# Encoder trunk on one core: sink negation moved behind the tables, tables begun with the third chunk of x, first slab cast first, products of zeros at the start

## The chip, the core and the metric

The kernel runs on one core of a Trainium2 chip. Time is device time in microseconds (us) of one execution; three executions of the kernel before gave 1385.47, 1386.06 and 1386.40 us, a median of 1386.06 us. One more execution was profiled.

Names used below: PE is TensorE's matmul side and PEld its weight loads; DVE is VectorE, ACT is ScalarE, POOL is GpSimd, SP is SyncE. Each engine works through its own instructions in the order in which the program issues them. DMAs are issued from queues of SP, ACT and POOL.

## What is computed

```python
def reference(x, positions, attn_norm_g, w_in, ..., w_down):       # x: (1, 512, 1024) float32
    cos, sin = rope_tables(positions)
    for l in range(2):
        h = rms_norm(x, attn_norm_g[l])
        z = jnp.einsum('bsd,dc->bsc', h, w_in[l])                  # 1024 -> 4352 columns
        qa, ka, va, qb, kb, vb, ga, gb = jnp.split(z, IN_SPLITS, axis=-1)
        ...                                                        # q/k norms, rope on the A branch
        ya = window_gqa(qa, ka, va, sink_a[l]) @ w_proj_a[l]       # softmax with a sink value per head
        yb = neighbourhood_attn(qb, kb, vb, rel_bias_b[l]) @ w_proj_b[l]
        x = x + (sigmoid(ga) * ya + sigmoid(gb) * yb) @ w_out[l]
        h = rms_norm(x, ffn_norm_g[l])
        x = x + (silu(h @ w_gate[l]) * (h @ w_up[l])) @ w_down[l]
    return x
```

## The kernel before

Every large product is made of three products in a reduced float32 format: an operand is cut into a high part and a low part, and high times high, high times low and low times high are added in PSUM. One such product with 512 moving columns is the unit of PE's work. ACT makes a high part (a copy with rounding), DVE makes the low part (a subtraction).

x is held in eight **chunks** of 128 columns of the model width (`KD = 8`), the weights in **slabs** of some rows and columns. Layer 0 begins with `token_matmul` (line 881) for the A queries: for each chunk k it calls `start(nrm, k)` through `begin`, and then makes the 12 products of that chunk (four blocks of tokens `b`, three products each). `begin(k+1)` is called right after the three products of block 0 of chunk k, so PE's order is: four transposes of chunk 0; three products (chunk 0, block 0); four transposes of chunk 1; nine products (chunk 0, blocks 1 to 3); three products (chunk 1, block 0); four transposes of chunk 2; and so on.

`start` (line 1174) for one chunk issues: four transposes of `xin[k]` on PE into a bank `at`; `first_parts(k)`, the cut of the weight rows of that chunk (ACT cast to the high part, DVE subtraction to the low part); an ACT activation that reads the transposes and gives the high part `nrm.xh[k]`; an ACT copy of them to `xT[k]`; a DVE operation (SCALAR_TENSOR_TENSOR) from `xT[k]` to the low part `nrm.xl[k]`; an ACT square and a DVE addition for the mean square. For chunk 0, `first_parts` stands behind the activation to `xh`; for all others ahead of it. The three products of block 0 need, in this order, (xh, weight high), (xh, weight low) and (xl, weight high).

The first slab (chunks 0 and 1) is loaded by ACT's queue in two halves, the next three slabs by POOL's queue (`first_load`, line 529); x is loaded chunk by chunk by SP's queue. POOL's queue carries, in this order, the positions, the B gains, slab 1, further B gains, slabs 2 and 3, the A gains `gqa`, the sink values `snk`, the rest of the constants `cst`, and then later slabs.

Beside the main order of the products run **chains**: generators with conditions (`Need`), issued whenever a dry run of the whole program (with a cost for each operation) finds the operands ready and the engine's backlog under a limit. The dry run thereby sets the order of instructions on each engine; the second run replays it. `issue` and `drive` (lines 394 and 413) do this at every yield of the main order. `chain_tables` (line 751) makes the rope tables: it converts the positions into `vec2`, negates the sink values into `nsnk`, transposes `vec2` on PE, forms angles from `cst`, and makes two tables `trig` by Sin on ACT, the first with a load of ACT's function table; all else is DVE work in small pieces. `chain_rope_tables` (line 789) then needs `trig` and `gqa`. `nsnk` is read first by the A heads' score operations.

`mm_bank()` gives PSUM banks in a rotation of four, `at_bank()` those of another four. The PE instruction with which the program begins is the transpose of `vec` (gains of the norms), then the transposes of chunk 0.

Of the kernel before, what the change touches and what calls it, by code (L numbers as in the profile page):

```python
# [12 lines left out]
F32 = mybir.dt.float32  # L13
# [3 lines left out]
ALU = mybir.AluOpType  # L17
AX = mybir.AxisListType

P = 128  # L20
# [4 lines left out]
NB = S // P  # L25
# [61 lines left out]
def by_columns(ap):  # L87

    return ap.rearrange("p (r cc c) -> p cc r c", r=8, c=8)


def held(ap):
    return ap.rearrange("p (cc r c) -> p cc r c", r=8, c=8)
# [116 lines left out]
def trunk(ctx: ExitStack, tc: tile.TileContext, a: dict, out: bass.AP, lay: Layout):  # L210
    nc = tc.nc
    PS = bass.MemoryType.PSUM
    cp = ctx.enter_context(tc.tile_pool(name="cp", bufs=1))
# [7 lines left out]
    def nm(s):  # L221
        uid[0] += 1
        return f"{s}_{uid[0]}"
# [21 lines left out]
    def act(dtype=F32):  # L245
        return buf([S], dtype)

    def mm_bank():
        return pm.tile([P, S], F32, tag="mm", name=nm("mm"))

    def at_bank():
        return pa.tile([P, S], F32, tag="at", name=nm("at"))
# [42 lines left out]
    def touch(aps, start, end):  # L295
        for x in aps:
            o = name_of(x)
            if isinstance(o, int):
                lay.touch(o, steps[0], start, end)

    class Engine:
# [3 lines left out]
        def __getattr__(self, name):  # L305
            f = getattr(self.eng, name)

            def call(*args, **kw):
                if not lay.dry:
                    f(*args, **kw)  # L310
                    return
                aps = [x for x in (*args, *kw.values()) if isinstance(x, bass.AP)]
                acc = kw.get("accum_out") if "accum_out" in kw else (args[7] if name == "tensor_tensor_reduce" else None)
                steps[0] += 1
                sources = aps if kw.get("start") is False else aps[1:]
                start = max([clock[self.key]] + [at_(name_of(x), self.key) for x in sources])
                if self.key == "dma":
                    start = max(start, clock["pe"] - 3.0)
                    if self.eng is nc.gpsimd:
                        clock["pool"] += 1.0  # L320
                    end = start + aps[0].free_size() * aps[0].shape[0] * 4 / 360e3
                    clock["dma"] = end
                    end += 2.0 if aps[1].space == bass.MemoryType.DRAM else 7.0
                    ready[name_of(aps[0])] = end, "dma"
                    touch(aps, start, end)
                    return
                end = start + cost(self.key, name, aps[0], aps)
                clock[self.key] = end
                ready[name_of(aps[0])] = end, self.key
                if acc is not None:  # L330
                    ready[name_of(acc)] = end, self.key
                touch(aps, start, end)

            return call

    T = Engine(nc.tensor, "pe")
    V = Engine(nc.vector, "dve")
    A = Engine(nc.scalar, "act")
    G = Engine(nc.gpsimd, "pool")
# [44 lines left out]
    chains, done = [], set()  # L384
# [156 lines left out]
    def first_parts(k):  # L541
        raw, h, lo = raws[k // 2][:, k % 2], highs[k // 2][:, k % 2], lows[k // 2][:, k % 2]
        A.copy(h, raw)
        V.tensor_tensor(lo, raw, h.bitcast(F32), ALU.subtract)
# [149 lines left out]
    vec2T = cp.tile([P, P], F32, tag="vec2T", name="vec2T")  # L694
    ones = cp.tile([P, 2], F32, tag="ones", name="ones")
    magic = cp.tile([P, 32], I32, tag="magic", name="magic")
    G.memset(vec2, 0.0)
    G.memset(ones, 1.0)
    G.memset(magic, 0x5F3759DF)
# [15 lines left out]
    posi = cp.tile([P, P], I32, tag="posi", name="posi")  # L715
# [14 lines left out]
    gqa = cp.tile([P, 2, DEPTH, HD], F32, tag="gqa", name="gqa")  # L730
    for i, n in enumerate(("q_norm_a", "k_norm_a")):
        GQ.dma_start(gqa[:, i], a[n].rearrange("l d -> (l d)").unsqueeze(0).to_broadcast([P, DEPTH * HD]))
    snk = cp.tile([P, DEPTH, 8], F32, tag="snk", name="snk")
    GQ.dma_start(snk, a["sink_a"].rearrange("l h -> (l h)").unsqueeze(0).to_broadcast([P, DEPTH * 8]))
    GQ.dma_start(cst[:, P:], a["consts"][:, P:])
    warm = cp.tile([P, 2], F32, tag="warm", name="warm")
    A.copy(warm, ones)
    ps = at_bank()
    T.transpose(ps[:, :32], vec, ident[:32, :32])
    V.tensor_copy(vecT, ps[:, :32])  # L740

    def gain(norm, k):
        c = 16 * (norm % 2) + 8 * (norm // 2) + k
        return vecT[:, c : c + 1]

    xT = [buf([S]) for _ in range(KD)]
    nsnk = cp.tile([P, DEPTH, 8], F32, tag="nsnk", name="nsnk")
    gb = cp.tile([P, DEPTH], F32, tag="gb", name="gb")
    trig = cp.tile([P, 2, NB, 32], F32, tag="trig", name="trig")

    def chain_tables():
        yield Need("dve", [posi, snk, gqa])
        V.tensor_copy(vec2[64:68], posi[64:68])
        V.tensor_scalar(nsnk, snk, -1.0, None, ALU.mult)
        yield Need("pe", [vec2], [at_slots])
        at_slots.take()
        ps = at_bank()
        T.transpose(ps[:, :P], vec2, ident)
        yield Need("dve", [ps])
        V.tensor_copy(vec2T, ps[:, :P])  # L760
        at_slots.give(clock["dve"])
        posf = vec2T[:, 64:68]
        V.scalar_tensor_tensor(gb, vec2T[:, 0:2], HD ** -0.5, vec2T[:, 2:4], ALU.mult, ALU.mult)
        v3 = lambda t: t[:, : NB * 32].rearrange("p (b f) -> p b f", b=NB)
        ang = v3(act())
        for b in range(NB):
            V.tensor_scalar(ang[:, b, :], cst[:, C_INV : C_INV + 32], posf[:, b : b + 1], None, ALU.mult)
        yield Need()
        for i, shift in enumerate((0.25, 0.0)):
            n, r = v3(act()), v3(act())  # L770
            V.tensor_scalar(n, ang, INV_2PI, shift, ALU.mult, ALU.add)
            V.tensor_scalar(n, n, ROUND_MAGIC, None, ALU.add)
            V.tensor_scalar(n, n, -ROUND_MAGIC, None, ALU.add)
            yield Need()
            V.scalar_tensor_tensor(r, n, -TWO_PI_1, ang, ALU.mult, ALU.add)
            V.scalar_tensor_tensor(r, n, -TWO_PI_2, r, ALU.mult, ALU.add)
            V.scalar_tensor_tensor(r, n, -TWO_PI_3, r, ALU.mult, ALU.add)
            yield Need()
            if shift:
                V.tensor_scalar(r, r, HALF_PI, None, ALU.add)  # L780
            V.tensor_scalar(r, r, PI_LO, -PI_LO, ALU.min, ALU.max)
            A.activation(trig[:, i], r, AF.Sin)
            yield Need()
        done.add("trig")


# [386 lines left out]

    def start(nrm, k):

        ps = at_bank()
        for b in range(NB):
            T.transpose(ps[:, P * b : P * b + P], xin[k][:, b, :], ident)
        if k:
            first_parts(k)  # L1180
        A.activation(held(nrm.xh[k]), by_columns(ps), AF.Copy, scale=gain(0, k))
        if not k:
            first_parts(k)
        A.copy(held(xT[k]), by_columns(ps))
        V.scalar_tensor_tensor(nrm.xl[k], xT[k], gain(0, k), nrm.xh[k].bitcast(F32), ALU.mult, ALU.subtract)
        sq = act()
        A.activation(sq, xT[k], AF.Square)
        if nrm.acc is not None:
            V.tensor_tensor(sq, sq, nrm.acc, ALU.add)
        nrm.acc = sq  # L1190
        if k == KD - 1:
            done.add("acc0")

    def layer(l):
# [158 lines left out]
        if l == 0:  # L1353
            spawn(chain_tables())
# [366 lines left out]
```

## Time and profile before

| | |
|---|---|
| three executions | 1385.47, 1386.06, 1386.40 us (median 1386.06) |
| the profiled execution's time | 1385.97 us |
| its span, first to last instruction | 1384.2 us |
| PE busy | 1370.9 us (99% of the span), 8042 matmuls |
| DVE, ACT, POOL busy | 910.6, 707.6, 317.8 us |

All times of the trace count from the start of the span. A line of the timeline has start, duration, engine, source line, operation, output and inputs, shapes, count and, in brackets, how long the engine had been idle before and what ended that. All operations are recorded on line 310, that of a helper, so one goes by the names of tiles: `mm` and `at` are PSUM banks, `arena` is any buffer of the big SBUF arrays. A matmul's duration includes its latency; the distance between starts tells how fast PE goes on.

### The profile page before, as it was taken

To read this page: it belongs to the slowest core of one execution; us is meant where nothing else is said; L and a number is where in the kernel's file an instruction comes from. 1 tells how busy PE (TensorE), PEld (TensorE's weight loads), DVE (VectorE), ACT (ScalarE), POOL (GpSimd) and SP (SyncE) were. 2 spreads that over 40 slices of the span, in tenths; PEclk is the share of its full clock that TensorE was granted. 3 is DMA by queue.
4 is the path that set the end of the run, shared out by engine and by line. 5 is a ranking of instruction groups with operands and counts; after the bars stand their busy time and mean duration, and the time that the engine had idled before them with its cause. 6 is when DMAs were issued, how large, how long until landed. Compare 5 with 4: busy or idle time off the path is not lost.

```text
span 1384.2 us, 20905 instructions
## 1 busy us (share of the span) xinstructions
PE 1370.9 (99%) x8042; PEld 1211.4 (88%) x8042; DVE 910.6 (66%) x1702; ACT 707.6 (51%) x1171; POOL 317.8 (23%) x326
## 2 busy tenths in 40 slices
PE   8999999999999999999999999999999999999998
PEld 6888888888899999999888888888889999999996
DVE  5875878555976657575648667784568757575663
ACT  6476767634643333343545675785356434343441
POOL 4542222310211110111353422223012111111110
PEclk9999999999999999999999999999999999999999
DMA  8998888874766483735899979879559483645645
GB/s 212 182 173 141 162 156 152 174 174 124 152 151 152 108 197 91 184 93 106 160 188 190 167 138 161 155 139 213 148 117 188 92 213 92 153 122 122 149 84 119
DMA packets 197332, 207.46 MB, mean 150 GB/s; under 512 B 25568, under 2 KB 167056, under 8 KB 197232
## 3 DMA queue, kind: packets, MB, share of 16 engines
q0 software_dynamic: 134976, 141.54, 54.8%
q1 hardware_dynamic: 61904, 64.04, 15.9%
q8 instruction: 63, 1.03, 0.3%
q10 hardware_dynamic: 352, 0.54, 0.1%
q14 instruction: 37, 0.30, 0.1%
HBM read 193.51 MB, written 2.10 MB: 141 GB/s over the span
## 4 chain that ended last, share of the span: by engine, by line
PE 94%; ACT 2%; DMA 1%; DVE 1%; issue 1%; POOL 0%; POOLq 0%; ACTq 0%
PE mm L310 73%; PE at L310 21%; ACT arena L310 2%; DVE arena L310 1%; DMA snk<-in_sink_a 0%; DMA vec<-in_q_norm_b 0%; DMA arena<-in_w_in 0%; ACT L310 0%; POOL posi L310 0%; POOL arena L310 0%; POOL vec L310 0%; ACT trig L310 0%; ACT sm L310 0%; DVE sm L310 0%; DVE den L310 0%
## 5 line engine op out<-in xcount | busy, mean ns | idle before, releaser
L310 PE MATMUL mm<-arena 128*128 128x512 f32 (+1 forms) x5568 | 1113.4, 355 | 2.2 <-ACT arena L310 1.3
L310 PEld LDWEIGHTS mm<-arena 128*128 128x128 f32 x5568 | 905.1, 190 | 137.2 <-DVE arena L310 3.7
L310 ACT CAST arena<-arena 128x1024 fp32r<-128x1024 f32 (+2 forms) x278 | 235.4, 869 | 221.9 <-DVE arena L310 215.8
L310 DVE TENSOR_TENSOR arena<-arena,arena 128x1024 fp32r<-128x1024 f32 (+2 forms) x268 | 262.1, 993 | 49.0 <-ACT arena L310 48.1
L310 PE MATMUL at<-arena 128*128 128x256 f32 (+1 forms) x1952 | 282.8, 289 | 0.4 <-DVE negm L310 0.4
L310 ACT ACTIVATE arena<-arena 128x1024 fp32r<-128x1024 f32 (+3 forms) x252 | 206.6, 843 | 137.7 <-DMA arena<-in_w_down 59.6
L310 PEld LDWEIGHTS at<-arena 128*128 128x128 f32 x1952 | 259.9, 191 | 13.6 <-DVE negm L310 1.4
L310 DVE TENSOR_TENSOR arena<-arena,mm 128x512 f32<-128x512 f32 x144 | 98.8, 686 | 241.8 <-PE mm L310 240.3
L310 POOL DMA_DIRECT2D arena<-in_w_in x163 | 162.6, 1376 | 302.9 <-ACT arena L310 272.7
L310 POOL DMA_DIRECT2D arena<-in_w_down x96 | 99.9, 1241 | 503.1 <-ACT arena L310 347.8
L310 DVE TENSOR_TENSOR arena<-arena 128x1024 f32<-128x1024 f32 (+4 forms) x196 | 158.0, 823 | 2.4
L310 DVE TENSOR_TENSOR arena<-at,arena 128x512 fp32r<-128x512 f32 (+4 forms) x158 | 104.2, 660 | 30.6 <-ACT arena L310 24.1
L310 ACT CAST arena<-at 128x512 fp32r<-128x512 f32 (+2 forms) x116 | 64.4, 555 | 63.3 <-PE at L310 62.0
L310 PE MATMUL at<-cst,arena 128*128 128x128 f32 x472 | 73.9, 276 | 1.9 <-issue 1.4
L310 ACT ACTIVATE arena<-arena,negm 128x256 f32<-128x256 f32 (+1 forms) x128 | 68.2, 534 | 14.5 <-DVE negm L310 12.5
L310 ACT COPY arena<-at 128x512 f32<-128x512 f32 (+1 forms) x68 | 39.6, 582 | 67.0 <-PE at L310 66.5
L310 PEld LDWEIGHTS at<-cst,arena 128*128 128x128 f32 x472 | 58.1, 141 | 11.9 <-issue 1.8
L310 DVE TENSOR_TENSOR arena<-mm,arena 128x512 f32<-128x512 f32 x72 | 49.1, 686 | 25.3 <-PE mm L310 25.1
L310 DVE CUSTOM_DVE_ANT_0 arena<-at,cst,nsnk 128x256 f32<-128x256 f32 (+1 forms) x64 | 34.4, 547 | 34.9 <-PE at L310 34.1
L310 ACT ACTIVATE arena<-arena,vecT 128x512 fp32r<-128x512 f32 x24 | 17.4, 726 | 54.5 <-DVE arena L310 54.1
L310 DVE CUSTOM_DVE_ANT_0 arena<-at,arena 128x256 f32<-128x256 f32 x64 | 26.3, 420 | 17.3 <-PE at L310 17.0
L310 POOL DMA_DIRECT2D arena<-in_w_up x8 | 8.2, 1030 | 126.5 <-PE mm L310 78.8
(68 smaller groups left out, 422.8 us busy)
## 6 DMA issues: line engine op xcount, KB each, us to landing
arena<-in_w_in POOLq DMA_DIRECT2D x99, 512.0 KB, 7.3
arena<-in_w_down POOLq DMA_DIRECT2D x80, 512.0 KB, 6.7
arena<-in_w_gate SPq DMA_DIRECT2D x20, 1024.0 KB
arena<-in_w_up SPq DMA_DIRECT2D x20, 1024.0 KB
arena<-in_w_in POOLq DMA_DIRECT2D x64, 256.0 KB, 6.3
arena<-in_w_proj_a POOLq DMA_DIRECT2D x16, 512.0 KB, 7.3
arena<-in_w_proj_b POOLq DMA_DIRECT2D x16, 512.0 KB, 7.4
arena<-in_w_out SPq DMA_DIRECT2D x16, 512.0 KB
```

The source lines that it names most:

```text
L310: f(*args, **kw)
```

## The change

Four edits at the start of the program:

1. `nsnk`, the negation of the sink values, goes from the second place of `chain_tables` to its end, with a condition of its own for `snk` and `gqa`; the chain's first condition is now the positions alone and a key `x2`.
2. That key is set at the beginning of `start(nrm, 2)`, so the chain may begin once the third chunk's transposes are about to be issued.
3. In `start` for chunk 0, `first_parts` comes ahead of the activation to `xh`, as for all other chunks.
4. A tile of zeros (the memory of `trig[:, 0]`, later a table) is set by POOL ahead of its other memsets. PE multiplies it with itself, 128 by 128 by 128 in plain float32, seven times ahead of the transpose of `vec` and three times behind the transposes of chunk 0, into a bank of `mm_bank()`.

```diff
+    trig = cp.tile([P, 2, NB, 32], F32, tag="trig", name="trig")
+    idle = trig[:, 0].rearrange("p b f -> p (b f)")
+
+    def turn_over(n):
+
+        ps = mm_bank()
+        for _ in range(n):
+            T.matmul(ps[:, :P], idle, idle, start=True, stop=True)
+
+    G.memset(idle, 0.0)
     G.memset(vec2, 0.0)
...
     A.copy(warm, ones)
+    turn_over(7)
     ps = at_bank()
     T.transpose(ps[:, :32], vec, ident[:32, :32])
...
-    trig = cp.tile([P, 2, NB, 32], F32, tag="trig", name="trig")
...
     def chain_tables():
-        yield Need("dve", [posi, snk, gqa])
+        yield Need("dve", [posi], keys=["x2"])
         V.tensor_copy(vec2[64:68], posi[64:68])
-        V.tensor_scalar(nsnk, snk, -1.0, None, ALU.mult)
         yield Need("pe", [vec2], [at_slots])
...
             A.activation(trig[:, i], r, AF.Sin)
             yield Need()
+        yield Need("dve", [snk, gqa])
+        V.tensor_scalar(nsnk, snk, -1.0, None, ALU.mult)
         done.add("trig")
...
     def start(nrm, k):
 
+        done.add(f"x{k}")
         ps = at_bank()
         for b in range(NB):
             T.transpose(ps[:, P * b : P * b + P], xin[k][:, b, :], ident)
-        if k:
-            first_parts(k)
+        if not k:
+            turn_over(3)
+        first_parts(k)
         A.activation(held(nrm.xh[k]), by_columns(ps), AF.Copy, scale=gain(0, k))
-        if not k:
-            first_parts(k)
         A.copy(held(xT[k]), by_columns(ps))
```

## Rows read from the trace of the kernel before

**Rows 1.** The page's first part: busy time, share of the span, instructions.
```profile
PE 1370.9 (99%) x8042; PEld 1211.4 (88%) x8042; DVE 910.6 (66%) x1702; ACT 707.6 (51%) x1171; POOL 317.8 (23%) x326
```
**Rows 2.** Waits of PE, whole span: total us, times, longest.
```profile
PE at L310 <- DMA vec<-in_ffn_norm_g: 4.3, 1, 4.3
PE mm L310 <- ACT arena L310: 1.3, 1, 1.3
PE mm L310 <- DVE arena L310: 0.7, 3, 0.3
```
**Rows 3.** Windows: length, busy per engine (count), granted clock, DMA share, GB/s.
```profile
4.74:9.12 4.38, 3.10 (x7) 1.71 (x8) 1.45 (x4) 2.93 (x5) 3.23 (x6) 1.00 1.06 303
9.12:14.44 5.32, 5.32 (x18) 4.32 (x17) 2.28 (x4) 2.41 (x4) 2.78 (x5) 1.00 1.07 360
14.44:18.72 4.28, 3.88 (x18) 2.65 (x17) 1.83 (x4) 2.31 (x4) 0.13 (x1) 1.00 1.26 322
18.72:21.91 3.19, 3.19 (x17) 2.65 (x16) 3.10 (x11) 2.52 (x4) 0.00 (x0) 1.00 0.80 149
25.21:28.92 3.71, 3.46 (x18) 2.59 (x16) 2.42 (x6) 3.51 (x7) 0.00 (x0) 1.00 1.23 238
32.43:36.33 3.90, 3.59 (x17) 2.53 (x16) 3.13 (x9) 3.49 (x7) 0.00 (x0) 1.00 1.23 240
36.33:76.00 39.67, 39.67 (x192) 33.12 (x193) 34.16 (x114) 19.36 (x34) 20.66 (x21) 1.00 0.97 184
```
**Rows 4.** Timeline of PE, narrow windows: product starts before and after 13.6 us.
```profile
12.53 1.05 PE L310 MATMUL mm<-arena 128*128 128x512 f32 x2
12.96 0.94 PE L310 MATMUL mm<-arena 128*128 128x512 f32 x2
13.74 0.63 PE L310 MATMUL mm<-arena 128*128 128x512 f32 x2
19.08 3.00 PE L310 MATMUL mm<-arena 128*128 128x512 f32 x12
```
**Rows 5.** Timeline, 0.7 to 9.4 us: chunk 0 on PE, ACT, DVE, POOL.
```profile
0.74 0.21 POOL L310 MEMSET vec<- 128x128 f32 x1 [0.29 <-POOLq L1707]
4.74 1.11 PE L310 MATMUL at<-cst,arena 128*128 128x128 f32 x4 [0.19 <-DMA arena<-in_x]
5.89 0.69 ACT L310 ACTIVATE arena<-at,vecT 128x512 fp32r<-128x512 f32 x1 [1.63 <-PE at L310]
6.48 0.61 ACT L310 CAST arena<-arena 128x512 fp32r<-128x512 f32 x1
7.14 2.18 PE L310 MATMUL mm<-arena 128*128 128x512 f32 x3 [1.28 <-ACT arena L310]
7.73 0.74 DVE L310 SCALAR_TENSOR_TENSOR arena<-arena,vecT,arena 128x512 fp32r<-128x512 f32 x1
8.53 0.29 PEld L310 LDWEIGHTS mm<-arena 128*128 128x128 f32 x1 [0.38 <-DVE arena L310]
```
**Rows 6.** DMA traffic of the first 5.5 us, ACT's queue: packets, MB, share.
```profile
q10 hardware_dynamic: 212, 0.29, 18.7%
```
**Rows 7.** Timeline around the sink's negation, and two products behind it.
```profile
12.79 0.29 DVE L310 CAST vec<-posi 4x128 f32<-4x128 int32 x1
16.89 0.17 DVE L310 TENSOR_SCALAR nsnk<-snk 128x16 f32<-128x16 f32 x1 [3.80 <-DMA snk<-in_sink_a]
18.38 0.51 PE L310 MATMUL mm<-arena 128*128 128x512 f32 x1 [0.16 <-DVE arena L310]
```
**Rows 8.** Timeline: chunk 2's cast, table load and second Sin on ACT.
```profile
12.26 0.62 ACT L310 CAST arena<-arena 128x512 fp32r<-128x512 f32 x1 [0.23 <-DMA arena<-in_w_in]
24.40 1.28 ACT L310 ACT_TABLE_LOAD   x1
32.80 0.31 ACT L310 ACTIVATE trig<-arena 128x128 f32<-128x128 f32 x1 [1.22 <-DVE arena L310]
```
**Rows 9.** Timeline: plain float32 products with one moving column.
```profile
36.33 1.02 PE L310 MATMUL at<-ones,arena 128*128 128x1 f32 x8 [0.31 <-DVE arena L310]
```

## The prediction

> **What bounds the kernel now.** I read the page's first part, then PE's waits, then windows cut at the chunks, then the timelines of the windows that are too long. PE is busy for 1370.9 of 1384.2 us [rows 1], so 13.3 us is all that can be won from idle time. PE's waits say where it is: one of 4.3 us for the gains in `vec`, 1.3 us for the first operands from ACT, 0.7 us for DVE [rows 2]; from 36.33 us on PE is busy without a gap, 39.67 of 39.67 us [rows 3]. So only the first 36 us matter, and there busy time misleads, because a matmul counts as busy at half speed too. I therefore take the distance between the first transposes of successive chunks (4 transposes and 12 products each), which are the edges of the windows: 4.38 (chunk 0), 5.32, 4.28, 3.19, and then 3.30, 3.71, 3.51 (the 3.71 has a row, the other two follow from the edges) and 3.90 to the products for the mean square at 36.33 [rows 3]. The best, 3.19 us, is a chunk in which nothing waits. Beyond it the first chunk lost about 1.2, the second 2.13, the third 1.09 and the last five 1.66 us.
>
> Why each lost it: (a) Products with 512 columns follow each other by 0.43 us at 12.53 and 12.96, that is 1.2 GHz; 12 of them take 3.00 us from 19.08 on, the last one's latency included, about 0.23 each and so 2.4 GHz [rows 4]. The two products from 13.74 already run at the faster spacing [rows 4]. The clock column shows 1.00 throughout [rows 3], so the spacing decides here. Before the rise PE had worked in pieces since 4.27 and without a wait of note since 8.53 [rows 5]. That is the second chunk's 2.13. (b) DVE stood 3.80 us at the negation for the sink's DMA [rows 7]; behind it lay chunk 2's weight subtraction and `xl`, and PE's third product of that block came only at 18.38 [rows 7]. That is most of the third chunk's 1.09. (c) In the last five chunks the Sin pieces sit between the chunks' work in ACT's order: a table load of 1.28, a second Sin that stood 1.22 us for DVE [rows 8].
>
> **The change part by part.** I go along the same edges.
>
> *To chunk 1's transposes (9.12 before).* Here the chain of chunk 0 decides, not PE. Before: `xh` at 5.89, cast of the weights at 6.48, first product 7.14, `xl` begun 7.73, third product 8.53 [rows 5]. After, ACT does the cast first and must wait for the slab's first half. When that lands no row shows: it was there by 6.48, as the cast didn't wait [rows 5], and ACT's queue had moved 0.29 MB by 5.5 us, its 0.26 MB half and the 16 KB of gains [rows 6]. So 5.5 to 6.48; I take 6.05, as a transfer's last bytes and its release lie some tenths apart. Then cast 6.05, `xh` 0.59 later at 6.64 (the step from 5.89 to 6.48), first product at 7.34, copy to `xT` 7.23 to 7.81, `xl` at 7.84, third product 0.80 behind it (8.53 less 7.73) at 8.64. At 2.4 GHz it and the step to the transposes take 0.33, where it took 0.59 before: chunk 1 at 8.97, **-0.15**. With the slab at 5.5 it is -0.7, at 6.48 +0.3.
>
> The zeros must fit ahead. POOL's memset of a tile of the same size takes 0.21 from 0.74 [rows 5]; PE can begin at about 1.1. A transpose of 128 columns is stepped by about 0.23 in chunk 0 (four in 1.11, the last with its latency) [rows 5]. A plain float32 product is recorded as two matmuls (eight for the four products with the column of ones [rows 9]); two such steps make 0.43 to 0.46 for one product of zeros at 1.2 GHz, four would make 0.85 to 0.92. I take 0.43, as rows 9 show two. Seven end at about 4.1, ahead of `vec` at 4.27; the three behind chunk 0's transposes end before 7.2, under ACT's wait. They cost nothing under this cover; each 0.1 us more for one product moves the first product by 1.0, once the 7.34 is passed.
>
> The Trainium skill ("FP8 and Floating Point Precision", TensorE Precision Notes) says that true float32 makes four passes through the array. By it the sum would be that of the fourth rival below; the two records per product [rows 9] don't settle how many passes one holds.
>
> *Chunk 1 to chunk 2 (5.32 before).* If the clock has risen by 9 us, this becomes 3.19: **-2.13**. If the zeros don't bring the rise forward, 0. Before, PE stood idle between 5.85 and 7.14 ahead of the first product and had begun at 4.27 [rows 2, 5]; after, it works from 1.1 with short pauses, so I take an early rise. Chunk 2's cast waits for slab 1 until 12.26 [rows 8], and its `xl` would be ready near 14.8, ahead of PE's need at 15.1: half a microsecond of cover and less, nothing paid.
>
> *Chunk 2 to chunk 3 (4.28).* DVE has no `nsnk` wait, and the tables' first piece (0.29 [rows 7]) falls behind chunk 2: 3.19, **-1.09**. `nsnk` (0.17) moves to the end of the tables; its DMA has landed by 16.89 [rows 7], so there it waits for nothing, and ahead of the A heads nobody reads it.
>
> *Chunks 3 to 7 (17.61).* The same DVE and ACT pieces lie one chunk later. The second Sin, which stood 1.22 us in ACT ahead of chunk 7's cast, then falls behind chunk 7. In return all pieces meet a PE that comes 3.4 us earlier. I take **-0.4**; bounds are -1.2 (three quarters of the 1.66 gone) and +0.5 (a further stall like those).
>
> *Nothing else.* POOL's DMAs start about 0.14 later; the only one that is waited for is slab 1, under its half microsecond. Two more banks in the rotation shift which bank a later product takes; the next pair takes banks read out during nine products (2.0 us). x's and the weights' transfers for chunk 3 and later lie more than 3 us ahead in their queues.
>
> **Sum**: -0.15 - 2.13 - 1.09 - 0.4 = -3.77 on the profiled execution's 1385.97 (span 1384.2 and 1.8 around it): 1382.2 us. The median of before is 1386.06, 0.1 away. Behind 36 us PE is packed, so a gain there reaches the end.
>
> **The rivals.**
> *First, a late rise*: the clock comes up with four products and four transposes of chunk 0 and 1 still slow. 4 x 0.2 + 4 x 0.1 = 1.2 less: 1383.4. For it: the rise depends on when PE began, and its place isn't in the program. The Trainium skill ("TensorE: Matmul & The Clock Gate", What's actually happening) says that the count of slow matmuls changes from run to run of the same kernel, 6, 11 or 14. By that the time would scatter between these two cases; the three times before, 0.93 us apart, allow for that but don't show it.
> *Second, the zeros do nothing for the clock* (the change doesn't do what it is built for): only the stall and the tables remain, -0.15 + 0.25 (the third product still slow) - 1.09 - 0.4 = -1.4: 1384.6. Against it: PE works 3 us more ahead of 4.27.
> *Third, given back on DVE*: behind the chunks DVE is busy for 34.16 of 39.67 us up to 76 us [rows 3]. If the heads there hang on DVE with no slack to the end of attention, the tables, no earlier in absolute time, hold them, and PE waits for what it won: 1386.0. Against it: PE had no such wait in that stretch [rows 3].
> *Fourth, slower*: the products of zeros take 0.85 each at 1.2 GHz. Seven end at 7.05, `vec` and the transposes of chunk 0 (1.3) at 8.4, three more at 10.9; the third product comes at 11.8 instead of 8.53. If the clock doesn't rise for them either, +3.3 stands against the -1.5 of stall and tables: 1387.8; with 0.95 each, +4.3 and 1388.8. It decides from about 0.67 per product on; beneath that even the slow clock leaves a gain.
>
> **How the numbers follow.** Forecast 0.60 (own range 1381.3 to 1383.2: the slab's bounds and those of chunks 3 to 7), first rival 0.18, second 0.09, third 0.07, fourth 0.06. A measurement of this kernel can tell about 0.2%, 2.8 us: the line is at 1383.3. Faster by more: nearly all of the forecast (0.57) and half of the first rival (0.09), 0.66. Slower by more: the heavier half of the fourth, 0.03. Within: the rest, 0.31. The range goes from 1381.3 to 1384.9: it takes in the first two rivals and leaves out the third and fourth and the rims.
>
> **What would show it.** In the profile after: products of zeros from about 1.1 to 4.1, at 0.43 or less; product spacing of 0.23 from chunk 0's blocks on (right) or 0.43 until 11 or 13 us (first, second rival); transposes of chunk 1 near 9.0, chunk 2 near 12.2, chunk 3 near 15.4, the products for the mean square near 32.6; no DVE wait of 3.8 us ahead of `nsnk`; the cast for chunk 0 at 5.5 to 6.5. The prediction falls if chunk 3 comes at 15.4 and the end doesn't move (third rival), if `vec` waits for the zeros past 4.3 (fourth), or if the slab lands later than 6.5.

## The result

The kernel after took 1388.08 us, the median of 22 executions (1386.99 to 1389.77); the kernel before took 1385.86 us in 22 (1385.19 to 1386.95). The ratio is 1.0016, its 95% interval 1.0010 to 1.0022: 2.2 us slower, where 3.8 us less was forecast. The profiled execution took 1388.03 us with a span of 1386.3; the forecast was made against 1385.97 and 1384.2.

The first part of after's page, and below it the first three of PE's waits over the whole span (us in total, times, longest):

```profile
PE 1371.9 (99%) x8062; PEld 1213.0 (87%) x8062; DVE 911.4 (66%) x1704; ACT 707.7 (51%) x1169; POOL 318.1 (23%) x327
```
```profile
PE mm L310 <- ACT arena L310: 3.3, 3, 1.7
PE mm L310 <- DMA arena<-in_w_down: 1.8, 2, 1.0
PE mm L310 <- DVE arena L310: 1.6, 3, 0.5
```

The wait of 4.3 us for `vec` [rows 2] is gone, since zeros fill it; PE's waits for ACT grew from 1.3 to 3.3 us and those for DVE from 0.7 to 1.6, and among the new kinds are two waits for `w_down`, a weight of the feed-forward part.

The windows of after, cut at the first transposes of successive chunks like [rows 3] (length, busy PE, PEld, DVE, ACT, POOL, granted clock, DMA share, GB/s):

```profile
4.64:8.74 4.10, 2.84 (x15) 2.17 (x14) 1.64 (x3) 2.31 (x4) 2.92 (x6) 1.00 1.04 301
8.74:11.94 3.20, 3.20 (x18) 2.65 (x17) 2.05 (x3) 2.38 (x4) 1.34 (x3) 1.00 1.06 354
11.94:15.25 3.31, 3.31 (x18) 2.59 (x16) 1.84 (x3) 2.83 (x5) 2.05 (x3) 1.00 1.07 331
15.25:18.55 3.30, 3.30 (x19) 2.71 (x18) 2.59 (x6) 1.80 (x3) 0.00 (x0) 1.00 1.27 342
18.55:24.55 6.00, 3.76 (x18) 2.54 (x17) 2.77 (x9) 3.77 (x6) 2.45 (x3) 1.00 0.54 99
24.55:27.76 3.21, 3.21 (x17) 2.64 (x16) 2.78 (x8) 2.55 (x4) 0.29 (x1) 1.00 1.12 185
27.76:32.88 5.12, 3.77 (x18) 2.54 (x17) 3.73 (x8) 4.50 (x8) 2.73 (x3) 1.00 0.83 157
32.88:36.75 3.87, 3.87 (x20) 3.26 (x19) 2.76 (x7) 3.21 (x5) 0.15 (x1) 1.00 0.75 172
```

Chunks 1, 2 and 3 begin at 8.74, 11.94 and 15.25, against 9.12, 14.44 and 18.72 before: 3.47 us ahead at chunk 3, as forecast (15.35). Then one chunk takes 6.00 us and another 5.12, and PE comes to the products for the mean square at 36.75, where before came at 36.33. The two are not the same place in PE's work: behind chunk 7's transposes stand 12 products ahead of them in before and 15 in after (timelines).

```profile
32.78 3.24 PE L310 MATMUL mm<-arena 128*128 128x512 f32 x12
```
```profile
33.23 3.68 PE L310 MATMUL mm<-arena 128*128 128x512 f32 x15
```

A mark that has the same work ahead of it in both is the 97th product of 512 columns, the first after the 96 of the eight chunks: it begins at 39.40 in before and at 39.04 in after. So of the 3.47 us there are 0.36 left.

Why, by the timeline of ACT, POOL and PE around these two chunks (start, duration, engine, operation, idle before and what ended it):

```profile
13.18 1.52 POOL L310 DMA_DIRECT2D arena<-in_w_in  x2
20.74 1.06 ACT L310 ACTIVATE arena<-arena 128x1024 fp32r<-128x1024 f32 x1 [3.02 <-DMA arena<-in_w_in]
21.70 0.60 ACT L310 CAST arena<-arena 128x512 fp32r<-128x512 f32 x1
22.94 0.73 PE L310 MATMUL mm<-arena 128*128 128x512 f32 x2 [1.71 <-ACT arena L310]
27.98 1.28 ACT L310 ACT_TABLE_LOAD   x1
29.82 0.31 ACT L310 ACTIVATE trig<-arena 128x128 f32<-128x128 f32 x1 [0.56 <-DVE arena L310]
30.04 0.60 ACT L310 CAST arena<-arena 128x512 fp32r<-128x512 f32 x1
31.28 0.74 PE L310 MATMUL mm<-arena 128*128 128x512 f32 x2 [0.83 <-ACT arena L310]
32.54 0.50 PE L310 MATMUL mm<-arena 128*128 128x512 f32 x1 [0.53 <-DVE arena L310]
```

In chunk 4 ACT stands 3.02 us for a load of `w_in`: it is to begin the low part of slab 4, the first slab of the A keys' weights, and chunk 4's own cast is queued behind that. (From slab 4 on `w_low` makes the low part: ACT copies the high part with its sign turned, and a DMA adds the weights.) POOL issues this load at 13.18 (13.05 before), so it lands no earlier than it did, while ACT now arrives 3 us sooner. In chunk 6 the load of ACT's function table and the first Sin, which itself waits 0.56 us for DVE, stand ahead of that chunk's cast; in before the same two stood ahead of chunk 5's cast (timeline of ACT):

```profile
25.85 0.31 ACT L310 ACTIVATE trig<-arena 128x128 f32<-128x128 f32 x1 [0.17 <-DVE arena L310]
26.07 0.60 ACT L310 CAST arena<-arena 128x512 fp32r<-128x512 f32 x1
```

What differs is when they came. In before the table load began at 24.40 [rows 8], 0.81 us ahead of chunk 5's transposes, and the cast came 0.86 behind these. In after the table load began 0.22 us behind chunk 6's transposes, and the cast came 2.28 behind these.

Further back the same places in the program serve as marks. The first scores behind a wait of 0.2 us for `negm` stand at 204.40 in before and at 203.57 in after:

```profile
204.40 0.51 PE L310 MATMUL at<-arena 128*128 128x256 f32 x2 [0.22 <-DVE negm L310]
```
```profile
203.57 0.51 PE L310 MATMUL at<-arena 128*128 128x256 f32 x2 [0.23 <-DVE negm L310]
```

So after is 0.83 us ahead there (0.5 more than at the 97th product; no run looks into why), and it ends 2.1 us behind. The two feed-forward parts lie between. The product of after that waits for `w_down` in layer 0 and the issue of the 1 MB load of `w_gate` ahead of it (timeline), and then the 256 KB loads of `w_down` from 360 to 392 us (the DMA view: count, KB each, median us from issue to landing):

```profile
381.06 0.37 SPq L310 DMA_DIRECT2D arena<-in_w_gate  x1
...
391.56 2.62 PE L310 MATMUL mm<-arena 128*128 128x512 f32 x16 [1.04 <-DMA arena<-in_w_down]
```
```profile
arena<-in_w_down POOLq DMA_DIRECT2D x5, 256.0 KB, 12.1
```

The same issue and loads in before, where nothing waits:

```profile
388.80 0.37 SPq L310 DMA_DIRECT2D arena<-in_w_gate  x1
```
```profile
arena<-in_w_down POOLq DMA_DIRECT2D x5, 256.0 KB, 9.0
```

The load of `w_gate` begins 7.74 us sooner, because the buffer that it fills came free sooner (in both traces SP's queue waits for a DVE operation, in after for one that ends that much earlier); the loads of `w_down` that PE needs next run beside it and land 3.1 us later. In layer 1 it is the same: `w_gate` at 1061.17 against 1067.62, and a wait of 0.79 us at 1071.41. Each time PE loses more than the wait shown, as the record of the product ahead includes its latency: two products start 1.44 us apart at 390.12 and 1.18 at 1070.23, where 0.23 is usual. Counted at the same product, after loses 1.31 us at the first place and 1.05 at the second, then 0.28 at 1122, where a weight load waits for `w_down` again, and 0.17 at 1176: from 0.83 ahead to 1.98 behind.

### The profile page after: what moved, and what is told of

Its sections match the earlier page's. It is cut to its first block, busy times and chain, and to the rows that moved or that the text cites. A ratio compares the mean times of both kernels' runs of the same rounds, so it can differ in the third digit from the quotient of the medians.

```text
span 1386.3 us, 20940 instructions
## 1 busy us (share of the span) xinstructions
PE 1371.9 (99%) x8062; PEld 1213.0 (87%) x8062; DVE 911.4 (66%) x1704; ACT 707.7 (51%) x1169; POOL 318.1 (23%) x327
## 3 DMA queue, kind: packets, MB, share of 16 engines
q8 instruction: 64, 1.05, 0.3%
## 4 chain that ended last, share of the span: by engine, by line
PE 91%; DMA 4%; issue 1%; DVE 1%; ACT 1%; POOL 1%; DVEq 0%; POOLq 0%; ACTq 0%
PE mm L310 71%; PE at L310 19%; DMA arena<-in_w_in 2%; DMA arena<-in_w_down 2%; ACT arena L310 1%; DVE arena L310 1%; POOL arena L310 1%; DVE sm L310 0%; POOL posi L310 0%; POOL vec L310 0%; DVEq L1727 0%; POOL cst L310 0%; ACT trig L310 0%; POOL trig L310 0%; ACT sm L310 0%
```

## The experiments

The change does not touch the feed-forward part. But buffers of the big arrays get their places from a packer (`Layout.pack`) that takes each buffer's time of life from the dry run of the whole program; another order of instructions at the start gives other lives and so other places, also far from the edits. So **theory 1** is: of the slowdown about 3 us is the new places, the rest of the change brings about 1 us. Its rival is that the new order itself brings the collision. **Theory 2** is for the start: the gain ahead of chunk 3 is given back at slab 4's load and at the Sin's place, each by its own part. Its rival is that PE's lead is lost to something else as soon as these are gone. A **third** question is what the products of zeros are worth.

In these kernels the helper's line is 368 instead of 310. "Old places" means that each buffer has the place that the buffer of the same allocating function and turn has in the kernel before; the few that would overlap are placed anew (two in x1, 66 in x2). Unless it is said otherwise, a run has 11 executions. The pieces of code show values where the kernels read them from options.

**Order and places, one at a time.** x1 has after's order in before's places, x2 before's order in after's places.

```diff
     lay = planned(RUN)
-    lay.pack()
+    other = planned(PLACES)
+    other.pack()
+    lay.pack_like(other)
```

> The changed kernel with its instructions in their own order, but with its buffers at the places in the arena that the kernel before gave them (two small buffers of the A keys' rope are placed anew). The profile after shows PE waiting at 390.1 and 1070.2 us for w_down slabs that landed 12.1 us after their issue instead of 9.0, while SP's w_gate load, which waits for its buffer to come free, began 7.7 and 6.5 us earlier. Theory 1 (places: the changed order made the packer choose other places, so that this load begins earlier and takes the DMA engines from w_down): w_gate goes at about 388 and 1067 again, the two waits (1.2 and 1.0 us with what lies around them, 2.8 us of excess in the two stretches) go, and the time is about 1385.3, 2.8 below the changed kernel, at or a little under the kernel before. Rival 1 (the order or the shift in time of the instructions brings the collision, whatever the places): the waits stay and the time is about 1388.1. Neither touches the first 40 us, which should look as in the profile after: chunk 3 near 15.3, the mean square's products near 36.7.

> The reverse: the kernel before, its instructions in their own order, with the buffers at the places that the changed kernel gives them, as far as they fit (66 of some 1600 are placed anew, all in attention and none of the feed-forward loads). Theory 1 (places): the w_gate load goes 6 to 8 us earlier than in the kernel before, PE waits for w_down near 391 and 1070, and the time is about 1388.6, 2.8 above the kernel before. Rival 1 (order or shift): no such wait, about 1385.9. The 66 buffers that were placed anew could add waits in attention, up to some tenths.

x1 took 1385.04 us (1384.66 to 1386.29), ratio 0.9993 (0.9984 to 1.0002): 3.04 less than after. x2 took 1387.84 (1386.94 to 1393.70), ratio 1.0016 (1.0007 to 1.0025), about what after itself shows. PE's wait for `w_down` in x2 (us in total, times, longest), its issue of `w_gate`, and that issue in x1 (timelines):

```profile
PE mm L368 <- DMA arena<-in_w_down: 1.7, 2, 1.4
```
```profile
381.78 0.37 SPq L368 DMA_DIRECT2D arena<-in_w_gate  x1
```
```profile
387.86 0.37 SPq L368 DMA_DIRECT2D arena<-in_w_gate  x1
```

The waits go with the places, not with the order: x2, which has none of the four edits, waits for `w_down`, and x1, which has all four, does not. The 256 KB loads of `w_down` take 12.2 us to land in x2 and 9.6 in x1. That `w_gate` is what delays them is argued from its place in time: no run moves this load alone, and `w_up`, loaded ahead of it, moves with the places too. What the edits themselves bring is x1's 0.9 us, and its interval reaches zero.

**The edits in two halves, in old places.** x3 has the first two (negation and tables), x4 the fourth (zeros); x9 is x4's program once more, and x10 has seven products of zeros and none behind chunk 0's transposes.

```diff
     A.copy(warm, ones)
-    turn_over(7)
...
-        if not k:
-            turn_over(3)
-        first_parts(k)
+        if k:
+            first_parts(k)
         A.activation(held(nrm.xh[k]), by_columns(ps), AF.Copy, scale=gain(0, k))
+        if not k:
+            first_parts(k)
```

That is x3 against x1. x4 and x9 take the zeros of the change and leave `chain_tables`, the key and the cast as before; x10 has no `turn_over(3)` besides.

> Only the move of the negation and the later begin of the tables, with the cast of chunk 0 and the start of PE as in the kernel before (no products of zeros), and the buffers at the places of the kernel before. Theory 2 (what PE wins in the first chunks is capped by ACT: the low part of slab 4 stands in ACT's order ahead of chunk 4's cast and can't begin before the slab lands at about 20.7; and the Sin with its table load now stands ahead of chunk 6): chunk 3 begins about 1.0 earlier than before (17.7 for 18.7), chunk 5 at about 24.5, the wait at chunk 6 comes as in the profile after, and the products for the mean square stand within 0.5 of the 36.3 before; time within 0.5 of the kernel before, 1385.5 to 1386.4. Rival 2 (the stall's 1.09 us reaches the end): 1384.8.

> Only the products of zeros (seven and three), with the negation ahead of the tables and the cast of chunk 0 as before, and the buffers at the places of the kernel before. Theory 3 (the two early gains are not additive: while DVE stands for the sink's DMA until 16.9, a faster PE only comes earlier to the same wait): chunk 2's transposes come near 12.1 instead of 14.4, chunk 3's no earlier than 18.3, and the time is within 0.5 of the kernel before, 1385.3 to 1386.3. Rival 3 (the clock's 2.1 us are worth their sum by themselves): 1383.7.

> The products of zeros alone once more, the same program as in the fourth experiment, which gave a median of 1387.71 us while its profiled execution took 1385.46. In that profile the clock rose to full at 5.5, was at half from 8.95 to 12.37 and full again. Theory 7 (the clock's place differs from execution to execution, so the worth of the zeros does too): the profile shows other stretches at half clock than those, by several us, and the executions again scatter over 2 us or more; the median lies between 1385.5 and 1388. Rival 7 (something fixed in this program costs 1.8 us): median again within 0.5 of 1387.7, and the profile shows the place.

> Of the products of zeros only the seven ahead of the gains' transpose, none behind chunk 0's transposes; all else as in the kernel before, at its places. If the three behind the transposes carry the early clock, it now rises late, as in the kernel before (13 to 14 us), and the time is near 1385.9. If the seven alone do it, the clock rises at 4 to 6 us as in five of six profiles with zeros so far. If what makes the fourth experiment slow in its timed executions lies in the three, this one is near 1385.9, if in the seven, near 1387.7.

> The same program as in the two runs with seven and three products of zeros in the order of before. Over those 22 executions the mean granted clock goes with the time: the six quickest (1385.4 to 1386.2) show 0.999 four times and 0.998 once or twice, the other sixteen (1386.8 to 1389.1) 0.998 or 0.997. This is one more look at a trace, in the hope of one of the slower executions. If the granted clock is the cause: an execution above 1386.8 us shows two stretches at half clock, or one that lies wholly under chunk 0's and chunk 1's products, its chunk 3 begins 1.5 us or more behind the 18.1 us of the two traces seen, and the windows behind 40 us are those of before to 0.1 us. If the cause lies elsewhere: chunk 3 begins near 18.1 us, and the 2 us are found behind 40 us or outside the span. If this execution is one of the quick ones (at most 1386.2 us), it tells nothing new.

x3 took 1385.17 us (1384.76 to 1386.38), ratio 0.9994 (0.9985 to 1.0003). x4 took 1387.71 (1385.46 to 1389.20), ratio 1.0009 (1.0000 to 1.0018), x9 1387.60 (1385.37 to 1389.13), ratio 1.0011 (1.0002 to 1.0020), x10 1386.19 (1385.74 to 1388.29), ratio 1.0003 (0.9995 to 1.0012). x12, x4's program in one more execution, took 1385.62.

x3 against x1: the zeros and the early cast bring chunk 3 forward from 17.39 to 15.17, and the time by 0.13 us. In x3 ACT waits 0.27 us for slab 4's load, in x1 2.92 us, and they go on within 0.42 us of each other:

```profile
20.13 1.06 ACT L368 ACTIVATE arena<-arena 128x1024 fp32r<-128x1024 f32 x1 [0.27 <-DMA arena<-in_w_in]
```
```profile
20.55 1.06 ACT L368 ACTIVATE arena<-arena 128x1024 fp32r<-128x1024 f32 x1 [2.92 <-DMA arena<-in_w_in]
```

The zeros without the first two edits win nothing either. In x12's trace the clock rose at 5.66 and chunk 2 began at 12.09, 2.35 us ahead of before, but chunk 3 at 18.33, only 0.39 ahead, with a wait of PE of 2.22 us for DVE between them: the sink's negation holds DVE until its DMA lands, whenever PE arrives.

That explains no loss, and x4 and x9 lost 1.8 and 1.7 us at the median, where 1385.3 to 1386.3 was expected of x4. The trace kept is that of one execution, each time one of the quickest (1385.46, 1385.37, 1385.62), and shows no loss. Each execution's mean granted clock is recorded: of the 22 of x4 and x9, five took 1386.2 us or less, four at 0.999 and one at 0.998; the other seventeen took 1386.95 or more, all at 0.998 or 0.997 (the text ahead of x12 says six and sixteen). A difference of 0.001 over a span of 1384 us is 1.4 us of full clock (an estimate), so more time at half clock would have about the size of the loss. But that is not shown: x4's kept trace has 0.998 as well, with half clock from 8.95 to 12.37, and lost nothing, and x1 has an execution at 0.997 that took 1385.0. With x10 within 0.4 us of before, most of the loss goes with the three products behind the transposes. How they bring it stays open. In x10's trace the clock rose at 5.93 without them, and was back at half from 9.35 to 12.76.

**Slab 4's low part and the Sin, later.** x5 lets the low part of slab 4 (and that of the slab behind it) fall due 3.3 us of work later, x6 holds the tables' last steps (clamp and Sin on ACT) until chunk 7 has begun, x7 does both. All three are x1 otherwise.

```diff
-        plan_pair(w_in, KA0, KD)
+        plan_pair(w_in, KA0, KD, later_l=3.3 if l == 0 else 0.0)
...
-            yield Need()
+            yield Need(keys=["x7"])
             if shift:
```

> The changed kernel at the old places (as in the first experiment, 1385.04 us), with one more edit: the low part of slab 4 (the first A key slab of layer 0) is due 3.3 us later, so that in ACT's order it stands ahead of chunk 5's cast instead of chunk 4's. Theory 4 (PE's gain is given back at chunk 4, because this ACT operation waits for its slab until 20.7 and the cast of chunk 4 stands behind it): chunk 5's transposes begin near 21.8 instead of 24.36, chunk 6's near 25.1; the Sin wait at chunk 6 stays (5.1 us to chunk 7, near 30.2); the mean square's products come near 34.1 instead of 36.58 and the time is near 1382.5. Rival 4 (what is won ahead of 36 us is given back behind it, on DVE in attention): the edges move as said, the time stays near 1385.0.

> The changed kernel at the old places, with one more edit: the last clamp and Sin of the first table wait until chunk 7 has been begun, so that no Sin and no load of the function table stand in ACT's order ahead of a chunk. Theory 5 (the second place where PE's gain is given back is chunk 6, where DVE's table pieces, the table load and Sin stand ahead of the cast): the wait of 2.4 us at chunk 4 stays (chunk 5 near 24.4), chunk 6 to chunk 7 takes 3.2 to 3.3 instead of 5.13, the mean square's products come near 34.6 instead of 36.58, and the time is near 1383.1. Rival 4 (given back in attention, the more so as the tables now end later): near 1385.0 or above.

> Both edits together, low part of slab 4 one chunk later and Sin behind chunk 7, with the products of zeros, at the old places. Theories 4 and 5: all chunks from 1 to 7 take 3.2 to 3.4, chunk 7 begins near 28.4, the mean square's products come near 32.3, and the time is near 1380.8, faster than both kernels. Rival 4: 1384 to 1385.

x5 took 1382.63 us (1382.12 to 1385.37), ratio 0.9980 (0.9972 to 0.9989); x6 1383.56 (1383.03 to 1384.84), ratio 0.9984 (0.9976 to 0.9993); x7 1382.95 (1381.98 to 1383.61), ratio 0.9979 (0.9970 to 0.9987). Against x1 that is 2.41, 1.48 and 2.09 us less. By the medians each part does by itself what theory 2 says. In x6 the way from chunk 6 to chunk 7 falls from 5.13 to 3.19 us. In x5 that from 4 to 5 falls from 5.87 to 3.21, but x5's trace does not show that the edit did it: the clock rose late there, at 13.92, and chunk 4 began at 21.28, when the slab had landed anyway. The trace that shows it is x11's below, with chunk 4 at 18.90 and chunk 5 3.22 us later. Together they bring no more than the first alone. x7's windows of chunks 0, 1 and 2 show where the rest is:

```profile
4.68:9.22 4.54, 2.91 (x15) 1.88 (x15) 1.87 (x4) 2.82 (x5) 3.10 (x6) 0.83 1.10 320
9.22:13.32 4.10, 4.10 (x17) 3.43 (x16) 2.27 (x4) 2.31 (x4) 2.50 (x5) 0.77 1.05 364
13.32:16.54 3.22, 3.22 (x18) 2.65 (x17) 1.50 (x4) 2.31 (x4) 2.04 (x3) 1.00 1.09 295
```

All later chunks take 3.20 to 3.45 us. But the granted clock is 0.83 and 0.77 in the first two windows: it had risen at 4.26 and fell back to half at 7.68, and PE had stood idle ahead of chunk 0's first product:

```profile
5.17 0.83 PE L368 MATMUL mm<-trig 128*128 128x128 f32 x6
7.36 0.98 PE L368 MATMUL mm<-arena 128*128 128x512 f32 x2 [1.35 <-ACT arena L368]
```

The 1380.8 that was expected for x7 took an early rise for granted.

**Zeros once slab and Sin no longer stand in the way.** x8 is x7 without any zeros, x11 is x7 with eight products behind the transposes in place of three.

```diff
         if not k:
-            turn_over(3)
+            turn_over(8)
```

> As the one before, without the products of zeros and their memset. Theory 6 (with the two later waits out of the way, the earlier clock is worth its full sum): chunk 2 begins near 14.2, chunk 3 near 17.4, the mean square's products near 34.4, and the time is near 1382.9, 2.1 above the one with zeros. Rival 6 (the products of zeros are worth nothing or cost something, as the 1387.71 of the kernel with zeros alone suggests): no slower than the one with zeros.

> The kernel with both later pieces (low part of slab 4, Sin) and zeros, with eight instead of three products of zeros behind chunk 0's transposes. In the profile with three, PE stood idle from about 5.8 to 7.4 and the clock fell to half at 7.7 until 11.1, so that the time was 1382.95 instead of the expected 1380.8. Theory 7 with that cover: at full clock eight take 1.7 us and end near 7, just ahead of the first product; the clock holds, chunk 2 comes near 12.1 and the time is near 1381.3. Against it: where the clock hasn't risen by then, eight take 3.4 us, hold the first product until about 9 and cost about 1.3: near 1383.5 or above.

x8 took 1382.71 us (1381.94 to 1383.49), ratio 0.9978 (0.9969 to 0.9987), 0.24 under x7: seven and three products are worth nothing at the median. By the spans alone x7 is ahead, with a median of 1380.4 against 1380.9; its time outside the span is longer. Six of x7's executions have a mean granted clock of 0.999 and spans of 1379.0 to 1380.4, the five at 0.998 or 0.997 have 1381.0. x11 took 1381.11 (1380.81 to 1382.35, 6 executions), ratio 0.9966 (0.9954 to 0.9978), 1.60 under x8, 4.76 under before and 6.97 under after, and 0.2 from what was expected. PE behind chunk 0's transposes (timeline), and the windows of chunks 0, 1, 2 and 4:

```profile
4.95 1.95 PE L368 MATMUL mm<-trig 128*128 128x128 f32 x16
7.59 0.74 PE L368 MATMUL mm<-arena 128*128 128x512 f32 x2 [0.69 <-ACT arena L368]
```
```profile
4.46:9.19 4.73, 3.51 (x24) 2.84 (x24) 1.64 (x3) 2.82 (x5) 3.31 (x6) 1.00 1.06 303
9.19:12.39 3.20, 3.20 (x18) 2.64 (x17) 2.05 (x3) 1.80 (x3) 1.08 (x2) 1.00 1.06 362
12.39:15.59 3.20, 3.20 (x18) 2.65 (x17) 2.05 (x3) 2.92 (x5) 2.75 (x4) 1.00 1.07 320
18.90:22.12 3.22, 3.22 (x18) 2.64 (x16) 2.81 (x10) 2.55 (x4) 0.00 (x0) 1.00 1.46 281
```

PE's pause ahead of the first product is 0.69 instead of 1.35 us, the clock rose at 4.23 and stayed, and chunks 1 and 2 take 3.20 us. In this trace the products for the mean square stand at 31.98, against 36.33 before.

All runs in one table: first transposes of chunk 3, the products for the mean square and the 97th product of 512 columns in the profiled execution (its own time beside them), and the median. In after, x1, x3 and x6 three more products stand ahead of those for the mean square; the 97th product has the same work ahead of it in all rows, but for the zeros.

| | places | chunk 3 | mean square | product 97 | profiled | median |
|---|---|---|---|---|---|---|
| before | own | 18.72 | 36.33 | 39.40 | 1385.97 | 1385.86 |
| after | own | 15.25 | 36.75 | 39.04 | 1388.03 | 1388.08 |
| x2 before's order | after's | 18.79 | 36.30 | 39.33 | 1388.29 | 1387.84 |
| x1 after's order | before's | 15.17 | 36.58 | 38.87 | 1385.08 | 1385.04 |
| x3 no zeros, cast late | before's | 17.39 | 36.17 | 38.46 | 1386.38 | 1385.17 |
| x4, x9, x12 zeros only | before's | 18.16, 18.07, 18.33 | 35.77, 35.77, 35.95 | 38.83, 38.79, 39.01 | 1385.46, 1385.37, 1385.62 | 1387.71, 1387.60 |
| x10 seven zeros only | before's | 18.93 | 36.54 | 39.60 | 1386.51 | 1386.19 |
| x5 slab 4 late | before's | 17.96 | 35.80 | 38.81 | 1385.26 | 1382.63 |
| x6 Sin late | before's | 15.66 | 34.56 | 36.85 | 1383.97 | 1383.56 |
| x7 both late | before's | 16.54 | 32.93 | 35.94 | 1382.99 | 1382.95 |
| x8 both late, no zeros | before's | 17.48 | 33.84 | 36.88 | 1383.08 | 1382.71 |
| x11 both late, 7 and 8 zeros | before's | 15.59 | 31.98 | 35.01 | 1382.35 | 1381.11 |

## Why the prediction was wrong

**To chunk 1: right.** The cast began at 5.88 (6.05 forecast), chunk 1 at 8.74 (8.97). The zeros cost what the two records of [rows 9] said, by this row of after:

```profile
1.00 3.35 PE L310 MATMUL mm<-trig 128*128 128x128 f32 x14 [1.00 <-POOL trig L310]
```

Seven products end at 4.35, at most 0.48 each with their latency (0.43 were forecast, 0.85 by the fourth rival); `vec` was transposed at 4.43, 0.16 later than in before. The fourth rival is out: it took a pass at 0.23 us, the step of the transposes. The four passes that the Trainium skill ("FP8 and Floating Point Precision", TensorE Precision Notes) gives for true float32 are not out with it, though the prediction ties the two together. Products of 512 columns follow each other by 0.43 us at the slow clock [rows 4]; 128 columns are a quarter of that, and four times 128 again 0.43 (an estimate from that row), so this trace agrees with four passes.

**Chunk 1 to 3: right, but not as a sum of two terms.** The forecast has -2.13 for the clock and -1.09 for the stall, and after is 3.47 ahead at chunk 3. Alone the terms are not worth that: chunk 3 is 0.39 ahead with zeros only (x12) and 1.33 with the tables' edit only (x3). The stall ends at a fixed time, so a clock that rises early only lengthens it, and the stall's going leaves the slow clock. The second rival (no help from the clock) took the two as separate and lands at 1384.6, near x3's 1385.17.

**Chunks 3 to 7: the step that failed first.** The forecast takes -0.4 with bounds of -1.2 and +0.5. The kernel after went from 3.47 ahead at chunk 3 to 0.36 ahead at the 97th product, +3.1 (+3.9 by the products for the mean square, the mark of the forecast, with three more products ahead of them). Its ground was that the transfers for chunk 3 and later "lie more than 3 us ahead in their queues". That was said of what the chunks themselves need. ACT's order at chunk 4 holds another operation, the low part of slab 4, whose load is issued at 13.05 and which in before met it landed. It had no wait in the rows that were read, and so no cover was worked out for it: x3 shows it at 0.27 us of waiting with a lead of 1.2 us. The second thing was seen, but only half: "the second Sin falls behind chunk 7" came true, but the first Sin and its table load moved too, from ahead of chunk 5's cast to ahead of chunk 6's, and they came 1.0 us later against that chunk's transposes. x6 prices that at 1.48 us, x5 the slab at 2.41, against x1.

**Behind 36 us: the step that failed second.** "PE is packed, so a gain there reaches the end" holds only with the order and the places left as they are. At 203 us after is 0.83 ahead; at the end it is 2.1 behind, and the runs put 3.04 us (after less x1) and 1.93 us (x2 less 1385.91, the before beside it) on the places. The rivals looked for a loss within attention; none had a transfer begun too early, hundreds of us from any edit. Had the places stayed, after would have been x1: 1385.04, just above the upper end of the range, for the failed step ahead of it. Of the 5.9 us between forecast and measurement 3.0 thus go to the places and 2.8 are what x1 misses as well.

**The clock: partly right.** It rose early in after (at 5.59, by the trace's record of the clock) and stayed up. It does not always: of the traces of x4's program one shows 5.54 with a fall back, one 9.20, one 5.66, and x5's, with the same ten products, 13.92. x5 gives a price: in that execution chunk 1 took 5.28 us, against 3.20 in after, and the whole 1385.26, against a median of 1382.63. The Trainium skill ("TensorE: Matmul & The Clock Gate", What's actually happening) says that the number of slow matmuls changes from run to run of one kernel; these traces agree. The forecast gave an early rise 0.60 and a late one 0.18, on the ground that PE works 3 us more ahead of 4.27. What it left out is PE's wait behind the zeros, ahead of chunk 0's first product. It is 0.95 us in x4, 1.35 in x7 and 1.28 in x10, in whose traces the clock fell back 0.3 to 2.3 us after it, and 0.73 in after, 0.86 in x1, 0.93 in x6, 0.69 in x11 and 0.61 in x12, where it stayed up. With x4 and x6 only 0.02 apart and one trace each, this is a tendency and not a rule.

## What to carry to other kernels

Where a planner derives buffer places from the order of instructions, any change of order is two changes; run the new order in the old places before judging it. A gain ahead of a transfer that starts at a fixed time is worth only the slack of that transfer: list for every load behind the edit when it lands and who stands behind its first reader, also where nothing waits yet. Two orders are compared at a place that has the same work ahead of it in both. Work that is to bring TensorE's clock up should reach as far as the first real products: x11, where it left 0.69 us, was 1.8 us faster than x7, where it left 1.35.

## What was not expected of the hardware

Beside a 1 MB load that began 7.74 us sooner, loads of 256 KB took 12.1 us to land instead of 9.0. With PE at work again the granted clock can be back at half after it had risen (0.77 on the mean from 9.22 to 13.32 in x7). The clock column reads 1.00 in the stretch ahead of the first recorded change, although products there follow each other at the slow spacing [rows 3, 4]; only a trace with a fall back shows lower figures. The time outside the span, 1.8 us in the profiled execution of before, was 2.0 to 3.1 in ten of x7's eleven executions and 1.7 to 2.1 in x8's; what lengthens it was not found.
